# Merge gate A interleaved with the recurrence heads, the last head's gates in the GeLU gate

## The chip, the cores and the metric

The kernel runs on one core of a Trainium2 chip. The metric is the device time of one execution in microseconds (us). The engines are named as the profile names them: PE is TensorE's matmul row (PEld its weight loads), DVE is VectorE, ACT is ScalarE, POOL is GpSimd, SP issues most of the transfers.

## The reference

One layer of a diffusion backbone on 512 latent tokens and 256 context tokens, width 1024, all in fp32. What matters here is the token mixer, and in it the columns of one combined projection:

```python
z_lat = einsum('btd,de->bte', h_lat, w_in)   # columns: Fourier | X | GeLU gate G | merge gate A | merge gate B
u = dwconv(z[..., X])                        # width 4, per channel, latent and context
r = sigmoid(einsum('bthi,hij->bthj', u, wa) + ba)     # 8 heads of 128 channels, 2 directions
i = sigmoid(einsum('bthi,hij->bthj', u, wi) + bi)
log_a = -8 * r * softplus(-lam);  a = exp(log_a)
b = sqrt(-expm1(2 * log_a)) * (i * u)
h_t = a_t * h_{t-1} + b_t                    # scans: context, then latent; forward and backward
y_rnn  = (gelu(z[..., G]) * (h_fwd + h_bwd)) @ w_lru
merge  = sigmoid(z[..., A]) * y_four + sigmoid(z[..., B]) * y_rnn
x      = x + g1 * (merge @ w_out)            # g1 from the adaLN modulation of c
```

After it come the routing and 16 SwiGLU experts (expert choice, 64 tokens each), and a final RMSNorm.

## The kernel before, in words

The program is written out by hand for each engine: every engine runs its instructions in the order in which the code issues them, and waits on semaphores between engines.

**Weights.** The mixer's weights come as tiles of 256 columns (1 MB, list `W`), in the order Fourier, four X tiles, four A tiles, four G tiles, and so on. `load_next()` issues the next transfer of the list `seq` on SP's queue into one of three `raw` buffers. `split(j)` makes two parts of a tile, a rounded one `wH` (a copy on ACT, or on DVE where the caller says so) and the rest `wL` (a subtraction on DVE), each in two halves. There are two buffers for `wH` and two for `wL`. Every product of the mixer is three matmuls per 128 rows of the contraction (`mm3`): high by high, high by low, low by high.

**Recurrence.** For each of the 8 heads `h` the code issues the X columns of the head (`zX`, L725 and L726: 24 matmuls of 512 latent columns and 24 of 256 context columns, in 8 steps `k`), then `conv(h)` on DVE, which makes `u`. The four gate products of the head *before* (`gate(h - 1, ...)`, L674 and L675, plain fp32) stand behind steps k = 4, 5, 6 and 7 of `zX`. Each gate product is followed by a Tanh on ACT (L677). Then `lru(h - 1)`: on ACT two Tanh, two Exp and two Sqrt, on DVE two products with `u` (L688), two products with the root (L698), on POOL two products (L699), on DVE three scans (L705 to L709), on POOL the sum into `yr` (L711). In even heads the split of the next X tile, with its copies on DVE, stands between the products and the scans.

**Merge gate A.** Behind all heads: 8 column tiles `zA` of 24 matmuls (L426), each ended by `a_evac`: a Tanh on ACT and a product into `y4` on DVE (L751). The gate products of the last head stand in the second of these tiles, `lru(7)` behind the fourth. Then the GeLU gate: 8 tiles `zG`, each ended by a GeLU on ACT, a product into `yr`, a rounded copy `gH` on ACT and a subtraction `gL` on DVE. Then merge gate B with the recurrent map, the output projection with the routing, and the experts, whose weights (768 KB a transfer) are fetched ahead into rings of buffers.

**adaLN.** Sixteen of the 24 column groups of the modulation are formed between the tiles: `ada_acc` reads one 1 MB tile and makes on DVE two partial sums of 8 products (L271, L273, L276). A later `ada_red` adds them up over the partitions with two matmuls (`adb`, L291), and DVE adds the result to `g1` (L293) and scales it (L294).

**PSUM.** Matmul results lie in four buffers of 128 x 1024 fp32: tag `z` has two (`zX`, half of the `zA` and `zG`), tag `g` two (gate products, `adb`, the other tiles). A tile in a buffer waits until the readers of the tile before it in that buffer are done. The builder picks the buffer when the code opens the tile.

Of the kernel before, what the change touches and what calls it, by code (L numbers as in the profile page):

```python
# [17 lines left out]
P = 128  # L18
D = 1024
# [57 lines left out]
def layer(ctx: ExitStack, tc: tile.TileContext, I, out):  # L77
# [18 lines left out]
    # ------------------------------------------------------------------ long-lived tiles  # L96
# [49 lines left out]
    # ------------------------------------------------------------------ weight stream of the mixer  # L146
# [6 lines left out]
    W += [(cols(w_in, D_F + 256 * i), 8) for i in range(4)]  # L153
    W += [(cols(w_in, D_F + 2 * D + 256 * i), 8) for i in range(4)]
# [5 lines left out]
    J_X, J_A, J_G, J_B, J_O = 2, 6, 10, 14, 22  # L160
# [4 lines left out]
    ada_at = {j: [p] for j, p in zip([J_A] + list(range(J_A + 2, J_O)), range(8, 23))}  # L165
    ada_at[J_O + 1] = [23]
# [133 lines left out]
    # ------------------------------------------------------------------ start: tokens, constants, adaLN of layer input  # L300
# [131 lines left out]
    # ------------------------------------------------------------------ constants of the recurrence  # L432
# [26 lines left out]
    # ------------------------------------------------------------------ Fourier columns, as the modulation arrives  # L459
# [84 lines left out]
    # ------------------------------------------------------------------ 2-D DFT of the Fourier group, by its symmetries  # L544
# [73 lines left out]
    # ------------------------------------------------------------------ Fourier map to the model width  # L618
# [28 lines left out]
    # ------------------------------------------------------------------ recurrent branch  # L647
# [65 lines left out]
    GATES = [(0, 0), (0, 1), (1, 0), (1, 1)]  # L713
    AT = {4: 0, 5: 1, 6: 2, 7: 3}
    load_gw(0)
    for h in range(H):
        if h % 2 == 0:
            w = SP.pop(J_X + h // 2)
        zf = f2(zt(f"zX{h}"))
        for k in range(KD):  # L720
            wH, wL = ch(w, k, h % 2)
            n = 0
            for a, b, bc in ((wH, hH, cH), (wH, hL, cL), (wL, hH, cH)):
                f, l = k == 0 and n == 0, k == KD - 1 and n == 2
                pe.matmul(zf[:, 512:1024], a, b[:, k, :], start=f, stop=l)  # L725
                pe.matmul(zf[:, 256:512], a, bc[:, k, :], start=f, stop=l)  # L726
                n += 1
# [25 lines left out]
    def last_gates(k):  # L753
        if k % 2:
            gate(H - 1, *GATES[k // 2])
        if k == 1:
            a_evac(0, zz_[0])
        if k == 4:
            split(J_A + 1)

    for i in range(4):
        w = SP.pop(J_A + i) if i < 2 else use(J_A + i)
        zz_ = []
        for c in range(2):
            z = ct(c if i else 0, "zA")
            zz_.append(z)
            zcols(w, z, c, None if i or c == 0 else last_gates)
        evacs = lambda: [a_evac(2 * i + c, zz_[c]) for c in range(0 if i else 1, 2)]
        if i == 1:
            lru(H - 1, pre=lambda: split(J_A + 2, dve.tensor_copy), mid=evacs)  # L770
            close_lr()
            close_hc()
        else:
            evacs()
# [561 lines left out]
```

## Time and profile before

| | |
|---|---|
| time of three runs | 1219.57 us median (1216.5, 1219.57, 1226.09) |
| span of the profiled execution | 1215.1 us, 4.5 us under the median; a time of its own is not listed |
| mean granted TensorE clock | 0.987 of full speed |
| busy share of the span | PE 94%, PEld 56%, DVE 46%, ACT 24%, POOL 9% |
| bytes read from HBM | 364.43 MB, 302 GB/s over the span |
| X columns and recurrence | 96.6 to 215.7 us |
| merge gate A | 215.7 to 273.1 us |
| GeLU gate | 273.1 to 319.7 us |
| gate B and recurrent map; output and routing | 319.7 to 412.6; 412.6 to 475 us |
| experts and final norm | 475 to 1215 us |

The stage times are the starts of the first matmul of each stage on the timeline, from the span's start. A share of busy time is a mean over stages that have different limits, so each stage is to be read by itself.

### The profile page before, as it was taken

How to read it: one execution, taken by the hardware profiler on the slowest of the kernel's cores; microseconds unless marked ns; L12 is line 12 of the kernel's file. 1: busy time of each engine (PE TensorE's matmuls, PEld its weight loads, DVE VectorE, ACT ScalarE, POOL GpSimd, SP SyncE). 2: the span in 40 equal slices, each digit the busy share in tenths (PEclk: the TensorE clock that was granted, in tenths of full speed). 3: DMA queues.
4: the chain of work that ended last, by engine and by line, in shares of the span. 5: the costliest groups of instructions: out<-in, count | busy, mean ns of one | idle time of the engine just before them, and what ended most of it. 6: DMA issues, size and time to landing. Idle time of an engine off the chain costs nothing. (4 is left out here: it accounts for less than half of the span.)

```text
span 1215.1 us, 16698 instructions
## 1 busy us (share of the span) xinstructions
PE 1145.7 (94%) x6873; PEld 684.3 (56%) x6891; DVE 564.3 (46%) x1053; ACT 286.2 (24%) x448; POOL 112.7 (9%) x118
## 2 busy tenths in 40 slices
PE   8989988899999999999999999999999899999886
PEld 4768766688888897545445454344344344344333
DVE  5556899987666665232332342232232232232024
ACT  5543777634322222101001001001001001001004
POOL 4254343210000000000000000000000000000002
PEclk9989988999999999999999999999999999999999
DMA  8912011154664595999999999999999999999996
GB/s 310 318 62 91 21 45 53 49 183 150 207 199 148 181 395 213 314 387 416 364 408 417 403 407 418 403 408 419 409 410 418 413 413 414 410 414 411 404 399 212
DMA packets 146155, 368.01 MB, mean 303 GB/s; under 512 B 8912, under 2 KB 61656, under 8 KB 145952
## 3 DMA queue, kind: packets, MB, share of 16 engines
q1 hardware_dynamic: 143408, 363.52, 78.1%
q0 software_dynamic: 1088, 2.18, 0.6%
q10 hardware_dynamic: 1584, 1.25, 0.4%
q8 instruction: 54, 0.88, 0.3%
q14 instruction: 21, 0.17, 0.0%
HBM read 364.43 MB, written 2.10 MB: 302 GB/s over the span
## 5 line engine op out<-in xcount | busy, mean ns | idle before, releaser
L1111 PE MATMUL U<-ew,g 128*64 128x384 f32 x928 | 168.6, 495 | 10.4 <-DMA ew<-in_w_up_e 10.0
L1111 PE MATMUL G<-ew,g 128*64 128x384 f32 x960 | 174.5, 493 | 2.1 <-DMA ew<-in_w_gate_e 1.6
L1130 DVE TENSOR_TENSOR x<-x,sc 128x512 f32<-128x512 f32 x120 | 77.1, 684 | 101.9 <-PE sc L1127 101.9
L1111 PEld LDWEIGHTS U<-ew,g 128*64 128x64 f32 x928 | 59.6, 136 | 93.9 <-issue 55.0
L1111 PEld LDWEIGHTS G<-ew,g 128*64 128x64 f32 x960 | 65.7, 136 | 81.2 <-issue 60.2
L1244 POOL TENSOR_TENSOR o<-x,ew 128x512 f32<-128x512 f32 (+1 forms) x8 | 7.8, 1004 | 938.2 <-ACT o L1240 938.2
L1206 PE MATMUL Y<-ew,wd 128*64 128x512 f32 x324 | 82.8, 595 | 5.6 <-DMA ew<-in_w_down_e 5.5
L1210 DVE SCALAR_TENSOR_TENSOR wc<-Y,gc,g 128x512 f32<-128x512 f32 x15 | 11.3, 751 | 160.5 <-PE Y L1206 160.5
L1206 PE MATMUL Y<-ew,wa 128*64 128x512 f32 x312 | 78.1, 599 | 7.8 <-DMA ew<-in_w_down_e 4.6
L1194 ACT COPY wa<-T 128x384 f32<-128x384 f32 x16 | 7.7, 479 | 255.4 <-PE T L1193 255.4
L230 DVE TENSOR_TENSOR wL<-raw,wH 128x1024 fp32r<-128x1024 f32 x48 | 62.9, 1340 | 2.0 <-ACT wH L229 1.6
L1206 PEld LDWEIGHTS Y<-ew,wd 128*64 128x64 f32 x324 | 24.3, 137 | 56.5 <-issue 41.5
L1167 ACT ACTIVATE wc<-G 128x768 f32<-128x768 f32 x16 | 13.0, 811 | 178.8 <-PE G L1111 178.8
L1083 PEld LDWEIGHTS xg<-wa,xn 128*128 128x128 f32 x448 | 51.1, 192 | 0.2
L1083 PE MATMUL xg<-wa,xn 128*128 128x128 f32 x448 | 51.2, 275 | 0.0
L1206 PEld LDWEIGHTS Y<-ew,wa 128*64 128x64 f32 x312 | 23.5, 136 | 48.6 <-issue 31.7
L1049 DVE TENSOR_SCALAR wc<-wa,score 128x128 bf16<-128x128 f32 (+3 forms) x63 | 23.9, 379 | 57.0 <-ACT wa L1042 57.0
L1213 ACT CAST wb<-wc 128x512 fp32r<-128x512 f32 x15 | 9.3, 617 | 169.3 <-DVE wc L1210 169.3
L674 PE MATMUL ga<-u,gw 128*128 128x512 f32 x64 | 36.0, 645 | 10.0 <-issue 9.9
L1127 PEld LDWEIGHTS sc<-wb 64*128 64x128 f32 x240 | 23.9, 184 | 35.9 <-issue 35.3
L229 ACT CAST wH<-raw 128x1024 fp32r<-128x1024 f32 x38 | 38.0, 1045 | 18.3 <-PE zO L426 9.9
L699 POOL TENSOR_TENSOR th<-tp,th 128x768 f32<-128x768 f32 x16 | 35.0, 2205 | 49.2 <-DVE tp L698 49.2
(360 smaller groups left out, 2191.2 us busy)
## 6 DMA issues: line engine op xcount, KB each, us to landing
ew<-in_w_gate_e SPq DMA_DIRECT2D x120, 768.0 KB, 13.3
ew<-in_w_up_e SPq DMA_DIRECT2D x116, 768.0 KB, 15.0
ew<-in_w_down_e SPq DMA_DIRECT2D x113, 768.0 KB, 15.0
raw<-in_w_ada SPq DMA_DIRECT2D x24, 1024.0 KB, 5.5
raw<-in_w_in SPq DMA_DIRECT2D x16, 1024.0 KB, 4.8
wd<-in_w_down_e SPq DMA_DIRECT2D x7, 768.0 KB, 12.5
we<-in_w_down_e SPq DMA_DIRECT2D x7, 768.0 KB, 12.9
wd<-in_w_up_e SPq DMA_DIRECT2D x6, 768.0 KB, 14.6
```

What stands on the lines that cost most here:

```text
L229: (copy or act.copy)(wH[:, a], raw[:, a])
L230: dve.tensor_sub(wL[:, a], raw[:, a], wH[:, a].bitcast(F32))
L674: pe.matmul(gf[:, 512:1024], gw[:, d, i, :], u[:, TC:TA], start=True, stop=True)
L699: pool.tensor_tensor(b, s, b, op=OP.mult)
L1049: dve.tensor_scalar(GT[c][:, 0:m], sB[:, 0:m], s, None, op0=OP.is_lt)
L1083: pe.matmul(a[k // 4][:, P * (k % 4) + q.start:P * (k % 4) + q.stop], XN[n // 2][:, n % 2, P * k:P * k + P], oh[:, n, q], start=n == 0, st ...
L1111: pe.matmul(t[64 * f:64 * f + 64, n, 0:384], xg[:, k, c:c + CAP], w[:, o:o + 384], start=k == 0, stop=k == KD - 1, tile_position=(0, 64 * f))
L1127: pe.matmul(a[dh][:, c], w, v, start=j == 0, stop=j == 1, tile_position=(64 * dh, 0))
L1130: dve.tensor_add(xs, xs, a[dh])
L1167: act.activation(v3(sl), G[:, :, 0:384], AF.Silu)
L1206: pe.matmul(yp[64 * dh:64 * dh + 64, :], hT[j // 3][:, j % 3, 64 * f:64 * f + 64], w[dh][:, i, :], start=kf == 0, stop=kf == 11, tile_posi ...
L1210: dve.scalar_tensor_tensor(y, yp, gc[:, e % 3:e % 3 + 1], g2, op0=OP.mult, op1=OP.mult)
```

## The change

The weight tiles are ordered X, A, X, A, ... Behind the X columns of head `h` follows one A tile of 128 columns, `zA[h]`, in a `g` buffer. Its `a_evac` stands behind step k = 3 of the next head's X columns, ahead of that head's gate products. The gate products of the last head stand in the first GeLU tile behind k = 1, 3, 5 and 7, its `a_evac` behind k = 0, and `lru(7)` behind that tile. All splits now copy on ACT; the split of an A tile stands at the head of an even head, that of the next X tile behind `conv` of an odd head. `ada_red` and `ada_acc` stand at the end of each odd head, behind `lru(h - 1)`, and then behind each pair of GeLU tiles as before; all 16 groups are done one place or more earlier, so that one `ada_red` and one `ada_acc` in the output projection fall away.

```diff
     W = [(cols(w_in, 256 * i), 8) for i in range(2)]
-    W += [(cols(w_in, D_F + 256 * i), 8) for i in range(4)]
-    W += [(cols(w_in, D_F + 2 * D + 256 * i), 8) for i in range(4)]
+    for i in range(4):
+        W.append((cols(w_in, D_F + 256 * i), 8))
+        W.append((cols(w_in, D_F + 2 * D + 256 * i), 8))
...
-    ada_at = {j: [p] for j, p in zip([J_A] + list(range(J_A + 2, J_O)), range(8, 23))}
-    ada_at[J_O + 1] = [23]
+    ada_at = {j: [p] for j, p in zip([J_X + 1, J_X + 3, J_X + 5, J_X + 7] + list(range(J_G, J_O)), range(8, 24))}
...
+    zA = {}
+
+    def tail_of(h, k, at):
+        if k == at[0] - 1:
+            a_evac(h, zA.pop(h))
+        if k in at:
+            gate(h, *GATES[at.index(k)])
...
     for h in range(H):
         if h % 2 == 0:
-            w = SP.pop(J_X + h // 2)
+            split(J_X + h + 1)
+            wx, wg = SP.pop(J_X + h), SP.pop(J_X + h + 1)
...
-            if h and k in AT:
-                gate(h - 1, *GATES[AT[k]])
+            if h:
+                tail_of(h - 1, k, (4, 5, 6, 7))
...
         conv(h, zf[:, 256:1024])
-
-        def next_split(h=h):
-            if h % 2 == 0:
-                split(J_X + h // 2 + 1, dve.tensor_copy)
+        if h % 2:
+            split(J_X + h + 1)
+        zA[h] = gt("zA")[:, 0, :]
+        zcols(wg, zA[h], h % 2)
         if h:
-            lru(h - 1, next_split)
-        else:
-            next_split()
+            lru(h - 1)
+        if h % 2:
+            ada_red()
+            ada_acc(J_X + h)
...
     for i in range(4):
         w = use(J_G + i)
         for c in range(2):
             z = ct(c, "zG")
-            zcols(w, z, c)
             j = 2 * i + c
+            zcols(w, z, c, None if j else lambda k: tail_of(H - 1, k, (1, 3, 5, 7)))
+            if j == 0:
+                lru(H - 1)
...
         if n == 1:
             ada_red()
-            ada_acc(J_O + 1)
...
-    ada_red()
```

DVE, `lru(3)` before, from the products with the root to the next `conv` (`tp3` and `th` are its tiles, `wL5` is the next weight tile):

```order
L698 SCALAR_TENSOR_TENSOR tp3_1385<-th0_3_1339,tp3_1385 128x768
L698 SCALAR_TENSOR_TENSOR tp3_1388<-th0_3_1361,tp3_1388 128x768
L229 CAST wH5_1399<-raw17_884 128x1024
L230 TENSOR_TENSOR wL5_1400<-raw17_884,wH5_1399 128x1024
L229 CAST wH5_1399<-raw17_884 128x1024
L230 TENSOR_TENSOR wL5_1400<-raw17_884,wH5_1399 128x1024
L705 SCALAR_TENSOR_TENSOR tp3_1385<-th0_3_1339,th1_3_1350 128x768
L707 SCALAR_TENSOR_TENSOR tp3_1388<-th0_3_1361,th1_3_1372 128x256
L709 SCALAR_TENSOR_TENSOR tp3_1388<-th0_3_1361,tp3_1388,th1_3_1372 128x512
L663 TENSOR_SCALAR u5_1483<-zX5_1411,col_80 128x768
```

The split stands ahead of the scans, and the next `conv` right behind them.

DVE in the changed program, `lru(2)`, which stands in odd head 3, from the same place on (`adb8` is the sum over the partitions, `acc9` the next `ada_acc`):

```order
L698 SCALAR_TENSOR_TENSOR tp2_1422<-th0_2_1343,tp2_1422 128x768
L698 SCALAR_TENSOR_TENSOR tp2_1425<-th0_2_1365,tp2_1425 128x768
L705 SCALAR_TENSOR_TENSOR tp2_1422<-th0_2_1343,th1_2_1354 128x768
L707 SCALAR_TENSOR_TENSOR tp2_1425<-th0_2_1365,th1_2_1376 128x256
L709 SCALAR_TENSOR_TENSOR tp2_1425<-th0_2_1365,tp2_1425,th1_2_1376 128x512
L293 TENSOR_TENSOR g1_94<-adb8_1440,g1_94 128x256
L294 TENSOR_SCALAR g1_94<-g1_94 128x256
L271 TENSOR_SCALAR acc9_0_1444<-raw20_1171,cs_91 128x256
L271 TENSOR_SCALAR acc9_1_1445<-raw20_1171,cs_91 128x256
```

The read of `adb8` now stands behind the scans. Six more `acc9` products, `L276`, both halves of the next A tile's `wL7`, the product `y4_3` of `zA[3]` and `conv(4)` follow in this order.

PE, the first gate product of the last head (`ga7`) before, in the second A tile (the semaphores that a row waits on are in brackets):

```order
L426 MATMUL zA_1735<-hH_99,wH6_1603 128x512 [waits DVE_49,PE_49]
L426 MATMUL zA_1735<-hL_100,wH6_1603 128x512
L426 MATMUL zA_1735<-hH_99,wL6_1604 128x512
L426 MATMUL zA_1735<-hH_99,wH6_1603 128x512
L426 MATMUL zA_1735<-hL_100,wH6_1603 128x512
L426 MATMUL zA_1735<-hH_99,wL6_1604 128x512
L674 MATMUL ga7_1742<-u7_1684,gw7_1578 128x512 [waits DMASW0_49,Activation_49]
```

Here the A tile waits for DVE (the `conv` that reads the same buffer), and the gate product for a Tanh on ACT.

PE in the changed program, the same product in the first GeLU tile, behind `zA[7]` and `adb10`:

```order
L291 MATMUL adb10_2003<-acc10_1_1728,ones_86 128x256 [waits Activation_49]
L426 MATMUL zG_2028<-hH_99,wH10_1952 128x512 [waits Activation_49]
L426 MATMUL zG_2028<-hL_100,wH10_1952 128x512
L426 MATMUL zG_2028<-hH_99,wL10_1953 128x512 [waits DVE_49]
L426 MATMUL zG_2028<-hH_99,wH10_1952 128x512
L426 MATMUL zG_2028<-hL_100,wH10_1952 128x512
L426 MATMUL zG_2028<-hH_99,wL10_1953 128x512
L674 MATMUL ga7_2037<-u7_1944,gw7_1819 128x512 [waits DMASW0_49,DVE_49]
```

The gate product now lies in the `g` buffer that `adb10` had, and its wait on DVE is for `g1<-adb10`; the other `g` buffer holds `zA[7]`.

The buffers of tag `g` that the builder picked (0 or 1, in the order of opening): head 2: gates 0 0 0 0, `zA[2]` 1. Head 3: gates 0 1 0 1, `zA[3]` 0, `adb8` 1. Head 4: gates 1 1 1 0, `zA[4]` 1. Heads 5 and 7 are as head 3 (`adb9` and `adb10` in 1), head 6 as head 4. In the GeLU gate: gates 1 1 0 1, the second GeLU tile 0, `adb11` 1, the fourth GeLU tile 0. So in head 4, 6 and the GeLU gate the first gate product waits for the read of `adb`, and in heads 3, 5 and 7 the second one for the `y4` product of the A tile before.

## Rows read from the trace of the kernel before

**Rows 1.** Windows by stage: length, busy us by engine, granted clock, DMA share, GB/s.

```profile
core 0: us, PE busy (x) PEld busy (x) DVE busy (x) ACT busy (x) POOL busy (x), PEclk, DMA share, GB/s
96.60:215.70 119.10, 109.05 (x499) 82.54 (x498) 100.33 (x107) 71.54 (x76) 49.92 (x39) 0.94 0.17 54
215.70:273.10 57.40, 52.96 (x215) 40.61 (x213) 50.93 (x64) 29.79 (x35) 12.27 (x7) 0.97 0.37 121
273.10:319.70 46.60, 46.60 (x206) 37.78 (x204) 34.35 (x66) 18.08 (x25) 0.00 (x0) 1.00 0.54 180
412.60:475.00 62.40, 61.44 (x534) 56.65 (x535) 40.38 (x96) 18.54 (x35) 0.00 (x0) 1.00 0.65 248
475.00:1215.00 740.00, 697.37 (x4494) 329.63 (x4508) 222.13 (x500) 72.94 (x150) 7.77 (x8) 1.00 1.00 395
```

**Rows 2.** Timeline of PE: start, length, instruction, idle time before it in brackets.

```profile
65.60 1.09 PE L556 MATMUL fb<-dc,zs 128*128 128x65 f32 x4 [5.81 <-DVE zs L495]
...
138.91 1.10 PE L674 MATMUL ga<-u,gw 128*128 128x512 f32 x2 [0.99 <-issue]
...
150.90 0.40 PE L725 MATMUL zX<-hH,wH 128*128 128x512 f32 x1
...
151.96 0.39 PE L725 MATMUL zX<-hH,wH 128*128 128x512 f32 x1
...
157.63 2.05 PE L674 MATMUL ga<-u,gw 128*128 128x512 f32 x2 [4.46 <-issue]
...
225.86 0.47 PE L426 MATMUL zA<-hH,wH 128*128 128x512 f32 x1 [4.19 <-DVE u L667]
...
256.05 0.40 PE L426 MATMUL zA<-hH,wH 128*128 128x512 f32 x1
...
261.65 0.40 PE L426 MATMUL zA<-hH,wH 128*128 128x512 f32 x1
```

**Rows 3.** Windows behind three of these waits.

```profile
65.60:73.10 7.50, 7.50 (x32) 6.48 (x32) 3.53 (x13) 3.73 (x8) 5.77 (x22) 0.50 0.00 1
139.00:140.00 1.00, 1.00 (x3) 0.52 (x4) 1.00 (x2) 1.00 (x1) 0.00 (x0) 1.00 0.00 0
157.63:162.16 4.53, 4.53 (x10) 3.03 (x11) 3.46 (x4) 4.49 (x5) 1.33 (x1) 0.51 0.00 0
162.16:164.50 2.34, 2.34 (x12) 1.68 (x11) 1.25 (x1) 1.31 (x2) 2.34 (x2) 1.00 0.00 0
```

**Rows 4.** Timelines of DVE and ACT, the first head's recurrence.

```profile
117.71 1.08 DVE L663 TENSOR_SCALAR u<-zX,col 128x768 f32<-128x768 f32 x1 [4.27 <-PE zX L726]
...
121.97 1.82 DVE L688 SCALAR_TENSOR_TENSOR th<-th,u 128x768 f32<-128x768 f32 x2
...
133.29 1.28 DVE L709 TENSOR_TENSOR_SCAN tp<-th,tp,th 128x512 f32<-128x512 f32 x1
...
119.00 0.91 ACT L677 ACTIVATE th<-ga,lru_c 128x768 f32<-128x768 f32 x1 [1.44 <-PE ga L675]
```

**Rows 5.** Timelines of DVE and ACT in merge gate A.

```profile
258.47 0.40 DVE L293 TENSOR_TENSOR g<-adb,g 128x256 f32<-128x256 f32 x1
...
259.99 2.35 DVE L230 TENSOR_TENSOR wL<-raw,wH 128x1024 fp32r<-128x1024 f32 x2
262.26 1.27 DVE L751 SCALAR_TENSOR_TENSOR y<-zA,y 128x512 f32<-128x512 f32 x2
263.46 0.60 DVE L271 TENSOR_SCALAR acc<-raw,cs 128x256 f32<-128x256 f32 x2
...
266.82 2.35 DVE L230 TENSOR_TENSOR wL<-raw,wH 128x1024 fp32r<-128x1024 f32 x2
...
262.35 1.99 ACT L229 CAST wH<-raw 128x1024 fp32r<-128x1024 f32 x2
```

**Rows 6.** Timelines of ACT and DVE in the GeLU gate, one tile's end.

```profile
284.68 0.58 ACT L787 ACTIVATE zG<-zG 128x512 f32<-128x512 f32 x1 [2.72 <-PE zG L426]
...
285.30 0.69 DVE L788 TENSOR_TENSOR yr<-zG,yr 128x512 f32<-128x512 f32 x1 [2.61 <-ACT zG L787]
...
286.02 0.62 ACT L789 CAST gH<-yr 128x512 fp32r<-128x512 f32 x1 [0.76 <-DVE yr L788]
```

More of the change, by code (lines that the diff above doesn't have):

```diff
@@ L159, in layer @@
     W += [(cols(I["w_out"][0], 256 * i), 8) for i in range(4)]
-    J_X, J_A, J_G, J_B, J_O = 2, 6, 10, 14, 22
+    J_X, J_G, J_B, J_O = 2, 10, 14, 22
     NW = len(W)
@@ L711, in lru @@
         pool.tensor_tensor(yr[:, h, :], tps[0][:, TC:TA], tps[1][:, TC:TA], op=OP.add)
[L713 to L716, printed above, removed]
-        if h % 2 == 0:
-            w = SP.pop(J_X + h // 2)
[L719 to L727, printed above, removed]
-            if h and k in AT:
-                gate(h - 1, *GATES[AT[k]])
-        if h + 1 < H:
-            load_gw(h + 1)
-        conv(h, zf[:, 256:1024])
-        def next_split(h=h):
-            if h % 2 == 0:
-                split(J_X + h // 2 + 1, dve.tensor_copy)
-        if h:
-            lru(h - 1, next_split)
-        else:
-            next_split()
     def zcols(w, o, c, tick=None):
@@ L751, in a_evac @@
         dve.scalar_tensor_tensor(y4[j][:, :], z, 1.0, y4[j][:, :], op0=OP.add, op1=OP.mult)
[L753 to L774, printed above, removed]
-        ada_red()
-        ada_acc(J_A + i)
-    gp, close_gp = sb("gp", "right")
-    gH = gp.tile([P, H, T], F32R, name="gH")
-    gL = gp.tile([P, H, T], F32R, name="gL")
+    GATES = [(0, 0), (0, 1), (1, 0), (1, 1)]
+    zA = {}
[4 more added lines that the diff above has]
+            gate(h, *GATES[at.index(k)])
+    load_gw(0)
+    for h in range(H):
+        if h % 2 == 0:
+            split(J_X + h + 1)
+            wx, wg = SP.pop(J_X + h), SP.pop(J_X + h + 1)
+        zf = f2(zt(f"zX{h}"))
+        for k in range(KD):
+            wH, wL = ch(wx, k, h % 2)
+            n = 0
+            for a, b, bc in ((wH, hH, cH), (wH, hL, cL), (wL, hH, cH)):
+                f, l = k == 0 and n == 0, k == KD - 1 and n == 2
+                pe.matmul(zf[:, 512:1024], a, b[:, k, :], start=f, stop=l)
+                pe.matmul(zf[:, 256:512], a, bc[:, k, :], start=f, stop=l)
+                n += 1
+            if h:
+                tail_of(h - 1, k, (4, 5, 6, 7))
+        if h + 1 < H:
+            load_gw(h + 1)
+        conv(h, zf[:, 256:1024])
+        if h % 2:
+            split(J_X + h + 1)
+        zA[h] = gt("zA")[:, 0, :]
+        zcols(wg, zA[h], h % 2)
+        if h:
+            lru(h - 1)
+        if h % 2:
+            ada_red()
+            ada_acc(J_X + h)
     for i in range(4):
@@ L784, in layer @@
             z = ct(c, "zG")
-            zcols(w, z, c)
             j = 2 * i + c
+            zcols(w, z, c, None if j else lambda k: tail_of(H - 1, k, (1, 3, 5, 7)))
+            if j == 0:
+                lru(H - 1)
+                close_lr()
+                close_hc()
+                gp, close_gp = sb("gp", "right")
+                gH = gp.tile([P, H, T], F32R, name="gH")
+                gL = gp.tile([P, H, T], F32R, name="gL")
             act.activation(z, z, AF.Gelu_apprx_tanh)
@@ L944, in layer @@
     dve.tensor_copy(bias, g[:, 0, 0:NE])
-    ada_red()
     dve.tensor_mul(wr[:, :, 0:NE], wr[:, :, 0:NE], s2.unsqueeze(2).to_broadcast([P, KD, NE]))
```

## The prediction

> **What bounds the kernel now.** I read the windows by stage first, then PE's timeline in the stages that the change touches, then the engines that PE waits for there.
>
> In the last stage, 740 us of experts, the DMA engines are busy all the time (share 1.00, 395 GB/s) and PE 697 us of it [rows 1]. The change touches nothing there, and its transfers are issued behind the first part of the output projection. So the question is only when the mixer ends; what is won or lost in it moves the end by as much.
>
> The stages of the X columns, gate A and the GeLU gate last 119.1 + 57.4 + 46.6 = 223.1 us. PE is the engine that is nearly full in all three, but it waits [rows 2]: per pair of heads 0.99 us in one and 4.46 us in the other, where a gate product needs `u` and DVE has not come to that `conv` (the 4.46 comes twice, one row stands), and 4.19 us at the second A tile, whose buffer `conv` still reads. After the long waits the granted clock is at half, 1.2 of 2.4 GHz, for a while: a gate product and an X step take 4.53 us, where the next pair takes 2.34 [rows 3], so each costs 2.2 more. That is 0.99 + 2 x 4.46 + 4.19 = 14.1 us of waits and 3 x 2.2 = 6.6 us of slow clock, **20.7 us** in all. It is the most that a better order of the same work can win here.
>
> **The work itself does not change.** An X step of six matmuls takes 151.96 - 150.90 = 1.06 us, so the X columns of a head 8.5; a gate product 2.34 - 1.06 = 1.28; an A or GeLU tile of 24 matmuls 261.65 - 256.05 = 5.60 [rows 2, 3]. A pair of heads with two A tiles and one `adb` (about 0.4, an estimate from its 256 fp32 columns beside the gate's 768) is 2 x (8.5 + 5.1 + 5.6) + 0.4 = 38.8 us. What counts is which waits stand in it.
>
> **What a wait is now made of.** The recurrence of one head is a chain through four engines. It starts when the X columns end (117.71, where `conv` starts), the last Tanh of the gates starts 1.3 later, and the last scan ends at 134.57: **16.9 us** after the X columns [rows 4]. DVE's own work ahead of it, `conv` and the products with `u`, is 4.3 + 1.8, and a split 2.3 [rows 4, 5]: 8.4, less than the chain needs to reach DVE, so the chain sets the time and not DVE's load. In an odd head the changed program puts two copies of a split on ACT ahead of this chain, 1.99 us [rows 5]: 18.8. Then comes the read of `adb`, 0.4 [rows 5]: **19.2 us** after the X columns of an odd head. In an even head no copy stands ahead: 16.9, and the `y4` product, 0.6 [rows 5], ends at **17.5**.
>
> **Odd head to even head (3 to 4, 5 to 6).** From the end of X(3) PE runs the fourth gate product 1.3, `zA` 5.6, `adb` 0.4 and five X steps 5.3: 12.6. There stands the first gate product, whose buffer was `adb`'s: it waits until 19.2, **6.6 us**, and everything behind it on PE, the other X steps, waits with it. The slow clock follows, 2.2. Three gates and three steps, 7.0, later X(4) ends, at 28.4. The fourth gate waits for `y4_3`, which is behind `ada_acc` (263.46 to 266.82, 3.4), a split (2.3) and its own 0.6 [rows 5]: 25.5, hidden.
>
> **Even head to odd head (4 to 5, 6 to 7).** 1.3 + 5.6 + 5.3, then the first gate and a step, 2.3: 14.5. The second gate waits for `y4_4` until 17.5: **3.0 us**. Whether the clock falls after it no row tells: after 0.99 us it stayed at full speed, after 4.46 it fell [rows 2, 3]. I take none: 3.0 is the difference of two long sums, and the shorter row kept its clock; the other end is 2.2. So a pair has 6.6 + 2.2 + 3.0 = 11.8 us of waits, where a pair before has 0.99 + 4.46 + 2.2 = 7.7; two pairs give 23.6.
>
> **Heads 1 to 3.** There is no `adb` yet, but `y4_1` stands behind scans 18.8, `ada_acc` 3.4 and a split 2.3: 25.1. PE comes to `zA[2]`, whose buffer it is, at 1.3 + 5.6 + 8.5 + 5.1 = 20.5, a wait of 4.6. `conv(2)` stands behind `y4_1` too, so the chain of that head is 3.8 late, and the second gate of head 3 waits another 2.2: **6.8 us**. The slow clock after the first wait would only shorten the second.
>
> **GeLU gate.** From the end of X(7): 1.3 + 5.6 + 0.4 and two steps of 0.7 = 8.7, then the gate that needs `adb10` read: 19.2, **10.5 us**, and 2.2 of slow clock. The third gate needs `y4_7` at 25.5 and comes later, 26.8: hidden. The fourth gate ends at 30.8, and `lru(7)`, with no X columns left to lie beside, 15.6 after that (119.00 to 134.57) at 46.4. The product of the first tile, its copy (285.30 to 286.64), the GeLU of the second (0.6) and its product (0.7) [rows 6] end at 49.0. PE has done the second tile and the third by 30.8 + 5.6 + 0.4 + 5.6 = 42.4, and the fourth lies in the second's buffer: **6.6 us**, and 2.2. Together 21.5.
>
> **What else moves.** In the output projection one `ada_acc` and one `adb` fall away; PE is busy 61.4 of 62.4 us there [rows 1], so only the `adb` counts, 0.5 us. `raw` transfers: three per pair of heads instead of mostly one, on a queue whose engines are busy 0.17 to 0.37 [rows 1], each issued a head or more ahead; no cost. POOL's own order is the same; a split no longer lies beside POOL's products, which shortens DVE's load and not the chain.
>
> **Sum.** New waits 6.8 + 23.6 + 21.5 = 51.9; old ones gone 20.7; 0.5 off: **+30.7 us**. The profiled span would be 1215.1 + 30.7 = 1245.8 us. It is 4.5 us below the median of the three runs, so against the median 1219.57 + 30.7 = **1250 us**.
>
> **Bounds.** If the clock came back at once behind all four long waits, 8.8 less: 1241. If it stayed low as after the 5.81 us wait (7.5 us at 0.50, 3.75 lost instead of 2.2 [rows 2, 3]), 6.2 more, and with the clock low after the two waits of 3.0 us 4.4 more: 1261.
>
> **Rival 1: the A tiles cover the recurrence, and it is faster.** All 20.7 + 0.5 us are won: 1198 us. It decides itself at one point: whether `adb` is read within 12.6 us of the odd head's X columns and `y4` within 14.5 of the even one's. For it: DVE has less to do per pair than PE (two times conv 4.3, products 3.6, scans about 5.2, split 2.3 and `y4` 0.6, with 0.4 and 3.4 for adaLN: 36 against 38.8), and the wait for `conv` is gone indeed, since 5.6 us of `zA` stand ahead of it. Against it: the two waits hang on the end of the chain, 16.9 us, which no load shortens. The Trainium skill (Perfetto Trace Analysis, Optimization Strategy) says that where the most-contended engine changes from regime to regime, interleaving the regimes may help; DVE is busy 100 of 119 us in the first and PE 53 of 57 in the second, and by this rule the time is this rival's. The same page (Matmuls) says that independent groups should rotate through different PSUM banks, so that the reading of one overlaps with the next; the 4.19 us wait bears it out, and it speaks against this order, where `adb`, `zA` and the gates share two buffers. With a free buffer for each the sum would be rival 1's as well.
>
> **Rival 2: smaller, but slower.** The builder's buffers hold, but the chain is shorter than in the first head, by 3 us: then 6.6 becomes 3.6 twice, 3.0 nothing twice, 10.5 becomes 7.5, and the clock falls less often: some 12 + 4 us less, 1234. What speaks against it is that the chain was measured in a head where nothing else was queued.
>
> **Rival 3: the delay is lost behind.** If the experts' weights were fetched as early as before, a late mixer would find full buffers, and PE, which has 740 - 697 = 43 us of slack there, could catch up: no change, 1219. Against it: these transfers are issued behind the mixer's own work, and 395 GB/s with a share of 1.00 leaves nothing to catch up with.
>
> **How the numbers follow.** The forecast as walked, with its bounds from 1241 to 1261, has 0.78; rival 2 0.10; rival 1 0.07; rival 3 0.05. Within 1%, 12 us, is about what a measurement of this kernel can tell from no change. Faster comes from rival 1; same from rival 3; slower from the rest. The range takes the bounds and half of rival 2: 1233 to 1263.
>
> **What would show it.** From the first `zX` to the first `zB` some 254 us instead of 223. Waits of PE: the gate product for DVE's `g1` at L293, two times about 6.6 and once about 10.5; for `y4` at L721, about 3 us in heads 3, 5 and 7, and `zA[2]` 4.6; the fourth `zG` about 6.6 for `yr`. Clock at half behind the long ones. No wait for `u`. The expert stage as long as before. I am wrong if the waits on L293 are absent or near 1 us, or if the stretch to `zB` is long but the end does not move.

## The result and the profile after

The changed kernel takes 1261.61 us (median of 4 runs, 1258.42 to 1261.98), the kernel before 1218.55 in the same session: ratio 1.0341, 95% interval 1.0311 to 1.0372, so 43 us slower. The profiled execution took 1261.37 us with a span of 1259.3, 44.2 more than the span before. The forecast was +30.7.

The two traces by stage, from the first `zX`, `zB` and `zO` and the last `zO` (us):

| | before | after | difference | forecast |
|---|---|---|---|---|
| up to the first `zX` | 96.7 | 98.8 | +2.1 | 0 |
| first `zX` to first `zB` (X columns, gate A, GeLU gate) | 223.0 | 259.4 | +36.4 | +31.2 |
| first `zB` to first `zO` | 93.0 | 93.0 | 0 | 0 |
| output projection, first to last `zO` | 55.0 | 60.6 | +5.6 | -0.5 |
| the rest (experts) | 747.4 | 747.5 | +0.1 | 0 |

The 2.1 us at the start are no effect of the change: the first `zX` began anywhere from 95.5 to 102.3 us in the executions profiled below. The windows of the changed kernel (length, busy us of PE, PEld, DVE, ACT, POOL, granted clock, DMA share, GB/s) for the X columns with gate A, the GeLU gate, the output projection and the experts answer to [rows 1]:

```profile
98.80:283.50 184.70, 160.70 (x695) 122.59 (x694) 129.16 (x158) 94.50 (x104) 50.90 (x40) 0.93 0.23 74
283.50:358.20 74.70, 56.93 (x224) 43.87 (x223) 51.80 (x79) 32.88 (x41) 10.89 (x6) 0.89 0.36 121
451.20:519.10 67.90, 64.33 (x533) 59.39 (x532) 36.80 (x86) 18.54 (x35) 0.00 (x0) 0.95 0.55 213
519.10:1259.10 740.00, 698.47 (x4510) 329.70 (x4508) 222.22 (x500) 72.87 (x150) 7.76 (x8) 1.00 1.00 395
```

The experts take the same 740 us at 395 GB/s: what the mixer lost is lost at the end. PE stands idle 24 us of the first stage and 18 of the GeLU gate, which had no idle time before, and the granted clock is 0.93, 0.89 and, in the output projection, 0.95, where it was 0.94 to 1.00 in these stages before.

PE's timeline of the changed kernel (start, length, instruction, idle time before it and what ended it) has these waits from the X columns to gate B, where [rows 2] had those for `u`:

```profile
140.66 1.12 PE L674 MATMUL ga<-u,gw 128*128 128x512 f32 x2 [0.80 <-ACT th L677]
151.43 0.79 PE L426 MATMUL zA<-hH,wH 128*128 128x512 f32 x1 [4.10 <-DVE y L721]
191.44 2.08 PE L674 MATMUL ga<-u,gw 128*128 128x512 f32 x2 [6.53 <-DVE g L293]
218.16 1.47 PE L674 MATMUL ga<-u,gw 128*128 128x512 f32 x2 [3.02 <-DVE y L721]
243.87 2.08 PE L674 MATMUL ga<-u,gw 128*128 128x512 f32 x2 [6.53 <-DVE g L293]
271.62 1.12 PE L674 MATMUL ga<-u,gw 128*128 128x512 f32 x2 [3.02 <-DVE y L721]
295.69 2.08 PE L674 MATMUL ga<-u,gw 128*128 128x512 f32 x2 [10.40 <-DVE g L293]
326.69 0.79 PE L426 MATMUL zG<-hH,wH 128*128 128x512 f32 x1 [7.38 <-DVE yr L776]
```

The waits for `u` are gone, as forecast, and in their place stand those of the forecast: `zA[2]` 4.10 (4.6), the first gate of heads 4 and 6 6.53 (6.6), the second gate of heads 5 and 7 3.02 (3.0), the first gate in the GeLU gate 10.40 (10.5), the fourth `zG` 7.38 (6.6). Only the 2.2 that the forecast had in head 3 did not come, and 0.80 in head 2 was not in it. They sum to 41.8 us, 27.7 more than the 14.1 before.

DVE's timeline of an odd head of the changed kernel shows the row in which the readers of PE's buffers stand. `conv(3)` starts at 172.34, when the X columns end:

```profile
189.78 1.28 DVE L709 TENSOR_TENSOR_SCAN tp<-th,tp,th 128x512 f32<-128x512 f32 x1
190.99 0.40 DVE L293 TENSOR_TENSOR g<-adb,g 128x256 f32<-128x256 f32 x1
191.42 1.14 DVE L294 TENSOR_SCALAR g<-g 128x256 f32<-128x256 f32 x1
...
193.01 2.45 DVE L273 SCALAR_TENSOR_TENSOR acc<-raw,cs,acc 128x256 f32<-128x256 f32 x6
...
195.83 2.35 DVE L230 TENSOR_TENSOR wL<-raw,wH 128x1024 fp32r<-128x1024 f32 x2
198.10 0.68 DVE L721 SCALAR_TENSOR_TENSOR y<-zA,y 128x512 f32<-128x512 f32 x1
```

The last scan ends at 191.06, 18.7 us after the X columns (forecast 18.8), `adb` is read at 191.39, and PE's gate starts at 191.44. The `y4` product ends at 198.78, 26.4 after the X columns, where the forecast had 25.5.

The windows behind the waits answer to [rows 3], at PE's granted clock (the first number after the busy times):

```profile
151.43:157.38 5.95, 5.95 (x14) 4.69 (x15) 5.91 (x10) 4.65 (x5) 0.00 (x0) 0.50 0.81 272
191.44:194.92 3.48, 3.48 (x7) 2.17 (x8) 3.48 (x8) 0.52 (x1) 0.97 (x1) 0.50 0.00 0
218.82:222.24 3.42, 3.42 (x11) 2.44 (x10) 0.00 (x0) 0.91 (x1) 0.06 (x1) 0.50 0.00 0
243.87:249.54 5.67, 5.67 (x12) 3.66 (x13) 5.63 (x12) 0.91 (x1) 0.97 (x1) 0.50 0.03 9
271.62:275.00 3.38, 3.38 (x13) 2.24 (x14) 0.00 (x0) 0.90 (x1) 0.71 (x1) 1.00 0.00 0
295.69:300.74 5.05, 5.05 (x10) 3.35 (x11) 5.02 (x11) 0.90 (x1) 0.97 (x1) 0.50 0.00 0
326.69:331.46 4.77, 4.77 (x11) 3.80 (x12) 4.10 (x11) 2.98 (x4) 0.00 (x0) 0.50 0.00 0
477.67:485.00 7.33, 7.33 (x37) 7.33 (x38) 3.13 (x5) 0.00 (x0) 0.00 (x0) 0.54 0.87 337
```

Up to gate B PE runs 28.3 us at half clock (the six windows with 0.50), a loss of 14.2, where the forecast had 8.8. With it the stretch is explained: 27.7 of waits + 14.2 - 6.6 of slow clock before = 35.3 of 36.4.

The last window is in the output projection, where nothing was foreseen. There `pb` is the first matmul that reads the router's weights `wr`. The timelines of SP and ACT, of before and then of after, show the issue of `wr` and of the first experts' weights `ew`; PE's row of the changed kernel stands last:

```profile
418.68 0.55 SPq L202 DMA_DIRECT2D raw<-in_w_ada  x1
423.39 0.38 SPq L190 DMA_DIRECT2D raw<-in_w_out  x1
423.81 3.88 SPq L856 DMA_DIRECT2D ew<-in_w_gate_e  x7
419.41 0.39 ACTq L863 DMA_DIRECT2D wr<-in_w_router  x1
```

```profile
457.47 0.37 SPq L190 DMA_DIRECT2D raw<-in_w_out  x1
457.89 5.12 SPq L844 DMA_DIRECT2D ew<-in_w_gate_e  x7
458.20 0.39 ACTq L851 DMA_DIRECT2D wr<-in_w_router  x1
477.67 3.06 PE L930 MATMUL pb<-wr,modc 128*128 128x16 f32 x16 [2.67 <-DMA wr<-in_w_router]
```

Before, an adaLN weight took the `raw` buffer that came free at 418.68; the last output weight waited until 423.39 for the next one, and SP came to the experts only 4.4 us after `wr` was issued, which landed 5.1 us after its issue. After, that adaLN weight is gone from SP's row, the last output weight takes the free buffer, and 7 transfers of 768 KB follow it, the first 0.3 us ahead of `wr`. The 64 KB are there some 19.5 us after their issue, by the end of PE's wait. PE waits 2.67 and then loses 3.4 of 7.33 us at clock 0.54: 6.0, about the 5.6 of the table.

### The profile page after: what moved, and what is told of

Its sections match the earlier page's. It is cut to its first block, busy times and chain, and to the rows that moved or that the text cites. A ratio compares the mean times of both kernels' runs of the same rounds, so it can differ in the third digit from the quotient of the medians.

```text
span 1259.3 us, 16718 instructions
## 1 busy us (share of the span) xinstructions
PE 1159.7 (92%) x6891; PEld 693.3 (55%) x6891; DVE 556.8 (44%) x1043; ACT 293.9 (23%) x457; POOL 112.4 (9%) x118
## 5 line engine op out<-in xcount | busy, mean ns | idle before, releaser
L230 DVE TENSOR_TENSOR wL<-raw,wH 128x1024 fp32r<-128x1024 f32 x48 | 58.2, 1251 | 1.6 <-ACT wH L229 1.6
L229 ACT CAST wH<-raw 128x1024 fp32r<-128x1024 f32 x48 | 47.9, 1045 | 17.8 <-PE zO L426 9.9
L677 ACT ACTIVATE th<-ga,lru_c 128x768 f32<-128x768 f32 x32 | 28.9, 902 | 88.0 <-PE ga L675 88.0
L1113 PEld LDWEIGHTS sc<-wb 64*128 64x128 f32 x240 | 23.9, 184 | 35.9 <-issue 35.3
## 6 DMA issues: line engine op xcount, KB each, us to landing
we<-in_w_down_e SPq DMA_DIRECT2D x7, 768.0 KB, 12.4
```

What stands on the lines that cost most here:

```text
L229: (copy or act.copy)(wH[:, a], raw[:, a])
L230: dve.tensor_sub(wL[:, a], raw[:, a], wH[:, a].bitcast(F32))
L677: act.activation(t, gf[:, 256:1024], AF.Tanh, bias=(hbi if i else hba)[:, 8 * d + h:8 * d + h + 1], scale=0.5)
L1113: pe.matmul(a[dh][:, c], w, v, start=j == 0, stop=j == 1, tile_position=(64 * dh, 0))
```

## The experiments

Ratios are against the kernel before in the same session (its medians 1219.35, 1219.46, 1219.8 and 1219.91), differences to the changed kernel against 1261.6. These differences cross sessions, between which the kernel before moved by up to 1.4 us (1218.55 to 1219.91). The stage times are those of each run's profiled execution.

| run | median us | ratio, 95% interval | `zX` to `zB` | output projection |
|---|---|---|---|---|
| changed kernel | 1261.61 | 1.0311 to 1.0372 | 259.4 | 60.6 |
| e1_router | 1256.33 | 1.0274 to 1.0315 | 258.6 | 54.6 |
| e5_ada (from before) | 1228.06 | 1.0046 to 1.0099 | 225.4 | 62.4 |
| e2_adb | 1248.67 | 1.0223 to 1.0255 | 244.8 | 60.4 |
| e3_y4 | 1233.87 | 1.0103 to 1.0147 | 231.8 | 60.4 |
| e4_both | 1234.96 | 1.0097 to 1.0155 | 232.3 | 61.0 |
| e8_gates_only | 1253.07 | 1.0206 to 1.0314 | 249.8 | 59.1 |
| e6_gates | 1231.58 | 1.0060 to 1.0119 | 229.7 | 60.4 |
| e10_even | 1222.60 | 1.0012 to 1.0043 | 222.2 | 60.5 |
| e11_warm | 1266.77 | 1.0348 to 1.0411 | 262.8 | 62.5 |
| e7_all | 1211.26 | 0.9907 to 0.9949 | 216.7 | 54.6 |
| e9_last | 1211.88 | 0.9918 to 0.9960 | 215.9 | 54.6 |
| e12_shift | 1209.77 | 0.9903 to 0.9944 | 210.3 | 54.6 |

### The output projection: e1_router and e5_ada

```diff
 e1, in the changed kernel
-    nc.scalar.dma_start(wr[:, :, 0:NE], I["w_router"][0].rearrange("(k p) e -> p k e", p=P))
+    nc.sync.dma_start(wr[:, :, 0:NE], I["w_router"][0].rearrange("(k p) e -> p k e", p=P))
 e5, in the kernel before
-    ada_at = {j: [p] for j, p in zip([J_A] + list(range(J_A + 2, J_O)), range(8, 23))}
-    ada_at[J_O + 1] = [23]
+    ada_at = {j: [p] for j, p in zip(range(J_A, J_O), range(8, 24))}
...
-            ada_acc(J_O + 1)
...
-    ada_red()
```

> The changed kernel, with the 64 KB load of the router's weights issued on SP's queue, ahead of the experts' weights, instead of on ACT's. Theory: the output projection is 5.5 us longer because SP is free earlier there (no adaLN weight stands in its row any more), so 7 expert transfers are issued 0.3 us ahead of the router's load and this one lands after them; PE waits 2.7 us for it and then runs at half clock. Expected: no wait of PE for wr, first zO to last zO 54 to 55 us instead of 60.3, the total 5 to 6 us below the changed kernel, about 1256. Rival: the end is set by the experts' transfers, which are issued at the same moment as before, so PE's wait in the output projection is made up behind it: the total stays at 1261.

> The kernel before, with one part of the change alone: the last adaLN weight is accumulated in merge gate A instead of in the output projection. Theory: SP has no adaLN weight to wait for in the output projection, issues the experts' weights before ACT issues the router's load, and PE waits for that load with a slow clock behind it. Expected: a wait for wr of 2 to 4 us in the output projection, first zO to last zO 59 to 61 us instead of 54.8, total 4 to 6 us above before, about 1223 to 1225. Rival: the move is free or saves the 0.5 us of adb on PE, as the prediction had it, and the 5.5 us belong to something else in the changed order: 1218 to 1219.

With the load ahead on SP's queue, `pb` no longer waits, the output projection takes 54.6 us, and the total falls by 5.3: the theory's 5 to 6. SP's timeline of this kernel:

```profile
458.95 0.37 SPq L851 DMA_DIRECT2D wr<-in_w_router  x1
459.37 5.01 SPq L844 DMA_DIRECT2D ew<-in_w_gate_e  x8
```

The other way round, moving the adaLN weight alone makes the kernel before 8.7 us slower, more than the 4 to 6 expected. PE's timeline of it shows why:

```profile
446.86 3.57 PE L941 MATMUL pb<-wr,modc 128*128 128x16 f32 x16 [3.45 <-DMA wr<-in_w_router]
```

The wait for `wr` is there, 3.45, and the output projection is 7.4 longer; 2.4 more lie in gate A, where one more weight is accumulated and PE waits 1.66 for it at an `adb` (267.83). Both runs say that the loss there is the order of issue of two transfers, made by a part of the change that removes work.

### What stands behind the scans: e2_adb, e3_y4, e4_both

What is given to `lru` as `mid` is issued between its products and its scans; `evac` is the Tanh and the `y4` product of an A tile.

```diff
 e2
         if h:
-            lru(h - 1)
+            lru(h - 1, mid=ada_red if h % 2 else None)
         if h % 2:
-            ada_red()
             ada_acc(J_X + h)
 e3: y4 alone (no a_evac in tail_of)
+        evac = lambda: a_evac(h, zA.pop(h))
-            lru(h - 1)
+            lru(h - 1, mid=lambda: (evac()))
 e4: y4 and adb
+            lru(h - 1, mid=lambda: (evac(), ada_red() if h % 2 else None))
```

> The changed kernel, with the read of adb moved on DVE ahead of the scans of the odd heads; y4 stays behind them. Theory: the waits come from all that is queued behind the scans, not from adb alone. With adb read about 13.2 us after the X columns the first gate of heads 4 and 6 waits only 0.7 us instead of 6.5, but then zA of that head comes at 20.9 us to a buffer that y4 gives back at 25.5 (4.6 us), conv of the next head stands behind that y4 as well, and the second gate of the next odd head waits 4.3 instead of 3.0: 9.6 us a pair, as now. In the GeLU gate 10.4 becomes some 4.5 at the first gate and some 8 for y4 at the fourth. Expected: waits for L293 under 6 us in all instead of 23.5, those for L721 up from 10 to 25 to 32 us, total within 8 us of the changed kernel's 1261. Rival: adb's place behind the scans is itself the cause: 13 + 10.4 us and the slow clock behind them go, total 1228 to 1235.

> The changed kernel, with the Tanh and the y4 product of each A tile moved ahead of the scans of the head that runs beside it; adb stays behind the scans. Theory: the order of DVE's queue costs more than PE's waits by line say. zA[2]'s wait (4.1 and slow clock) and the two of 3.0 go; the first gate of heads 4 and 6 now gets the buffer of y4 (ready about 13.3 us after the X columns, 12.6 when PE comes), and adb's buffer is wanted by the third gate, at 17.3 against 19.4: 2 us instead of 6.5. In the GeLU gate 4.6 for y4 and about 5 for adb instead of 10.4, and 7 for yr as now. Expected: 22 to 30 us below the changed kernel, 1231 to 1239. Rival: each wait belongs to its own line, so only those for y4 go (4.1 + 6.0 and 4.6 of slow clock): 1247. Second rival: DVE becomes the bound of a pair of heads, conv comes late, and less than 10 us are won.

> The changed kernel, with the y4 product of each A tile and, in odd heads, the read of adb ahead of the scans (the two moves of the earlier experiments together). Theory: with y4 moved, what is left of the waits for adb is small (1.6 us where y4 alone was moved), and now DVE's queue is the limit: the split of the A weights comes late by 6.0 us in three places, and reading adb ahead of the scans makes DVE's odd head no shorter. Expected: within 4 us of the kernel with y4 alone moved, 1230 to 1238, with PE waiting for wL at L230. Rival: the two moves add up, 13 us more as adb alone brought: 1221.

With `adb` alone moved, 12.9 us are won, more than the 8 at most expected and less than half of what the rival had. PE's timeline of that kernel in heads 4 and 5, and DVE's in head 5:

```profile
197.83 0.79 PE L426 MATMUL zA<-hH,wH 128*128 128x512 f32 x1 [4.15 <-DVE y L721]
213.15 1.12 PE L674 MATMUL ga<-u,gw 128*128 128x512 f32 x2 [0.41 <-DVE y L721]
```

```profile
203.68 1.82 DVE L698 SCALAR_TENSOR_TENSOR tp<-th,tp 128x768 f32<-128x768 f32 x2
```

The wait moved on to `y4`, as the theory had it (4.15 against 4.6), but the second gate of the next head hardly waits (0.41 against 4.3): `conv(4)` starts late, at 197.69, and `y4_4` ends at 213.10, 15.4 us later and not 17.5. ACT had run ahead meanwhile: DVE goes into L698 without a wait, where in the changed kernel it waited 1.97 us for ACT at this place (208.72). POOL had not; it waits for DVE in both. So part of a delay on DVE is made up in the next head, which neither theory had. The waits for `y4` sum to 15.8 us, where the theory had 25 to 32.

With `y4` alone moved, 27.7 us are won, in the expected range and over the first rival's. Moving both wins no more (1235.0 against 1233.9). PE's timeline of e4 around head 4, and DVE's:

```profile
182.08 1.12 PE L674 MATMUL ga<-u,gw 128*128 128x512 f32 x2 [0.75 <-DVE y L721]
193.30 0.50 PE L426 MATMUL zA<-hH,wL 128*128 128x512 f32 x1 [2.17 <-DVE wL L230]
```

```profile
189.19 2.46 DVE L273 SCALAR_TENSOR_TENSOR acc<-raw,cs,acc 128x256 f32<-128x256 f32 x6
...
192.03 2.35 DVE L230 TENSOR_TENSOR wL<-raw,wH 128x1024 fp32r<-128x1024 f32 x2
```

The first gate, now in the buffer of an A tile, finds it within 0.75 us, and now `zA` waits 2.17 for its own weights' split, which stands behind `ada_acc`. So the second rival of e3, DVE as the bound, is there too, but small. No run gave the gates, `zA` and `adb` a buffer each, which the prediction names as another way to the same end; that stays untested.

### The last head's gates: e8_gates_only and e6_gates

```diff
+        last = None
+        if h == H - 1:
+            def last(k):
+                if k == 3:
+                    lru(h - 1)
+                if k >= 4:
+                    gate(h, *GATES[k - 4])
-        zcols(wg, zA[h], h % 2)
+        zcols(wg, zA[h], h % 2, last)
 GeLU gate, first pair of tiles: both zcols, then
+            lru(H - 1, mid=lambda: (product(0), product(1)))
 product(c) is the GeLU and the product with yr; e6 has e4's moves as well
```

> The changed kernel, with the second part of the change undone: the last head's gates run in its own A tile (after X step 3 of it), its recurrence beside the first two GeLU tiles, whose products with yr stand ahead of its scans; the X, A order and the places of y4 and adb stay. Theory: the 10.4 us wait for adb and the 7.4 for yr with their slow clock (22.7 in all) go, but DVE has both recurrences of the last heads, an adaLN weight and three splits in a row there, so zG1 waits some 1.5 us for y4, zG2 as much for its split, and zG4 some 6 us for the split of its weights, with the clock low behind it: 8 to 14 us won, 1247 to 1254. Rival: the GeLU gate's loss was the place of these gates alone, and all 22.7 go: 1239. Second rival: the recurrence of the last head is only moved, and nothing is won: 1258 to 1262.

> All three moves in one: y4 and adb ahead of the scans, and the last head's gates in its own A tile. Theory: against the kernel with y4 and adb moved the GeLU gate loses its waits for y4, adb and yr (about 16 us with the slow clock) and gets one for the split of zG4's weights (6 and slow clock): 1218 to 1226. Rival: DVE is the bound from the last X columns to the end of the GeLU gate, and no more than 4 us are won over the two moves alone.

e8 gives 8.5 us, inside the expected 8 to 14, though its four runs lie 15 us apart (1243.1 to 1258.1), and it is there by luck and not by the theory: `zG1` and `zG4` do not wait, and the waits for `adb` and `yr` are gone, but PE waits 6.17 us at the second of these gates. In e6 the same wait stands, and only 3.4 us are won over e4 (the intervals overlap), which is the rival's figure, though its cause (DVE) was another. ACT's timeline of e6:

```profile
263.51 1.28 ACT L695 ACT_TABLE_LOAD   x1
264.80 1.58 ACT L695 ACTIVATE tp<-tp 128x768 f32<-128x768 f32 x2
266.39 1.28 ACT L677 ACT_TABLE_LOAD   x1
267.69 0.90 ACT L677 ACTIVATE th<-ga,lru_c 128x768 f32<-128x768 f32 x1
```

I had put head 6's recurrence ahead of head 7's gates on ACT; the first gate's Tanh, whose buffer the second gate needs, stands behind all of it and two table loads. A row on ACT did what DVE's did in the changed kernel.

### Where adaLN is accumulated: e10_even and e7_all

```diff
-    ada_at = {j: [p] for j, p in zip([J_X + 1, J_X + 3, J_X + 5, J_X + 7] + ...
+    ada_at = {j: [p] for j, p in zip([J_X, J_X + 2, J_X + 4, J_X + 6] + ...
-        if h % 2:
+        if h % 2 == 0:
             ada_acc(J_X + h)
 e10: e4 with this; e7: e6 with this and with e1's edit
```

> The kernel with y4 and adb ahead of the scans (1235), and the adaLN weights of the heads accumulated in even heads instead of odd ones; the gates of the last head stay in the GeLU gate and the router's load on ACT's queue. Theory: the waits of three A tiles for the split of their weights (7.7 us) stood behind the 3.4 us of ada_acc in DVE's row; with it moved they go, and with them what PE loses behind: 8 to 13 us, 1222 to 1227. Rival: DVE's sum per pair is the same, so the waits move to conv or y4 of the other head: 1231 to 1235.

> As the one before, and the adaLN weights of the heads accumulated in even heads (DVE has 16.5 us of work there and 26 in odd ones), and the router's load on SP's queue ahead of the experts' weights. Theory: the router's load gives 5.3 as it did alone, and the evened load takes away most of the waits for the split of A weights, 3 to 8 us: 1206 to 1216, under the kernel before. Rival: DVE's sum over a pair of heads is what counts, not how it is spread, so only the router's 5.3 are won: 1214 to 1220, no different from before.

e10 is 12.4 us under e4, at the good end of what was expected: no tile waits for `wL` any more, and from first gate to first gate a pair of heads takes 39.85 us (135.41, 175.26, 215.12), where the forecast counted 38.8 of PE's work. e7 has it with the router's load and the gates in gate A: 1211.26, 20.3 under e6, of which the output projection's 5.8 is e1's. Its time lies in the expected range by luck: that range was set while e6 was expected at 1218 to 1226 and the edit at 8 to 13 us, and both were off. The 16.5 and 26 us of the expectation are the lengths of DVE's row in an even and an odd head; its work there in e4 is 13.6 and 23.0. e7 is the first that beats the kernel before, by 0.7%.

### Is it the clock: e11_warm

```diff
+            if h in (4, 6) and k == 4:
+                warm(26, zt("warm"))
             if h:
                 tail_of(h - 1, k, (4, 5, 6, 7))
 and warm(42, zt("warm")) ahead of the first gate in the GeLU gate
```

> The changed kernel, with matmuls on a constant put ahead of the three gate products that wait for adb (26 in heads 4 and 6, 42 in the GeLU gate, some 0.22 us each): they fill most of the 6.5, 6.5 and 10.4 us in which PE stands still and compute nothing that is used. Theory: the clock falls because PE stands still there, and the time lost behind these waits (1.75, 2.7 and 2.5 us, half of the stretch at half clock) comes back: 5 to 7 us below the changed kernel, 1254 to 1257. Rival: what follows is set by the recurrence's chain and not by PE's clock, so a faster PE only waits longer at the next place: 1260 to 1262.

The time came out above both ranges: 1266.8, 5.2 over the changed kernel. PE's timeline of this kernel in heads 4 to 7, and then the third gate product of head 4 in the changed kernel:

```profile
194.61 1.12 PE L674 MATMUL ga<-u,gw 128*128 128x512 f32 x2 [0.85 <-DVE g L293]
202.01 1.12 PE L674 MATMUL ga<-u,gw 128*128 128x512 f32 x2 [2.24 <-DVE y L721]
222.14 2.07 PE L674 MATMUL ga<-u,gw 128*128 128x512 f32 x2 [3.00 <-DVE y L721]
...
276.75 2.08 PE L674 MATMUL ga<-u,gw 128*128 128x512 f32 x2 [3.00 <-DVE y L721]
```

```profile
198.02 1.13 PE L674 MATMUL ga<-u,gw 128*128 128x512 f32 x2
```

The clock stayed at 1.00 through the filled waits, but in heads 4 and 6 the run does not test the theory, because with the edit the tiles lie in other buffers. The third gate product waits 2.24 us for `y4` at 202.01; in the changed kernel it started at 198.02, before that `y4` product ended (198.78), so there it cannot have lain in the same buffer. From first gate to first gate, heads 4 and 5 take 54.6 us instead of 52.4 and heads 6 and 7 54.6 instead of 51.8. Part of this is the third gate's wait; the rest is the clock, which in this execution fell behind both waits of 3.00 (0.50 in windows of 3.86 and 4.25 us from 222.14 and 276.75), where in the changed kernel it fell behind one of two.

In the GeLU gate the third gate product shares its buffer with `y4` in both kernels. There PE, with the clock kept up, comes earlier and waits 1.78 for `y4` and again 7.38 for `yr`, so that from the first gate to the fourth `zG` it takes 30.7 us instead of 31.0: of the 2.5 that the window of 5.05 us had cost, 0.3 came back. So the rival is right there; what the slow clock costs in heads 4 and 6 stays open. Of the whole, `zX` to `zB` is 3.4 longer, and 1.9 are in the output projection, which this edit does not touch: it took 60.4 to 62.5 us in the runs from the changed kernel that left the router's load as it was and the last gates in the GeLU gate.

### Toward a better order: e9_last and e12_shift

The diff shows the main lines.

```diff
 e9: e10 with e1's edit; the first pair's products ahead of lru(H - 1)'s scans, and
+            zcols(w, z[c], c, None if i or c else lambda k: tail_of(H - 1, k, (4, 5, 6, 7)))
 e12: e9 with one adaLN weight less in the GeLU gate
-    zip([J_X, J_X + 2, J_X + 4, J_X + 6] + list(range(J_G, J_O)), range(8, 24))
+    zip([J_X, J_X + 2, J_X + 4, J_X + 6] + list(range(J_G + 1, J_O)), range(8, 23))
+    ada_at[J_B] = [15, 16], the later ones one place on
+            if i + c == 0:
+                ada_red()
+                ada_acc(J_B)
```

> The fastest so far (1211), with the last head's gates back in the first GeLU tile, at its last four steps, and the products of the first two GeLU tiles still ahead of that head's scans. Theory: in its own A tile these gates waited 4.3 and 1.6 us for ACT, which has the head before's recurrence in its row; in the GeLU tile they wait some 3 us for y4, the 7.4 for yr do not come back, and zG4 may wait up to 2.7 for its split: 2 to 6 us won, 1205 to 1209. Rival: the last head's recurrence then starts 6 us later, and the GeLU gate waits for it as in the changed kernel: 1214 to 1218.

> The kernel before this one (1212, gates in the first GeLU tile), with one adaLN weight taken out of the GeLU gate: the first of the four is accumulated one place later, and merge gate B, where DVE is busy 29 of 42 us, takes two in its first pair of tiles. Theory: the wait of 5.6 us at the small adb product of the GeLU gate (PE waits for ada_acc, which stands behind the last head's scans and two gL products on DVE) goes, and DVE comes to the split of zG4's weights 3.4 us earlier: 4 to 8 us won, 1204 to 1208. Rival: DVE's backlog at the end of the recurrence is what counts, and the wait moves to a split, a product with yr or gate B: 1209 to 1213.

e9 is no faster than e7. The wait for `yr` did not come back, so the rival is wrong too; PE waits 2.55 for `y4` as expected and then 5.61 for an adaLN weight's sum, which no theory named and which e10 has too (6.98). Its timeline, then that of e12:

```profile
258.80 1.13 PE L674 MATMUL ga<-u,gw 128*128 128x512 f32 x2 [2.55 <-DVE y L721]
288.70 1.01 PE L287 MATMUL adb<-ones,acc 128*128 128x1 f32 x4 [5.61 <-DVE acc L276]
```

```profile
286.98 0.50 PE L429 MATMUL zG<-hH,wH 128*128 128x512 f32 x1 [2.39 <-ACT wH L232]
```

e12 takes that wait away, and `zX` to `zB` falls by 5.6 to 210.3 us, but the medians differ by 2.1 only (1209.77 against 1211.88, with overlapping intervals). The time lies in the rival's range. The trace bears out both in part: the named wait is gone, as the theory had it, but `zG` now waits 2.39 for its split, and from `zB` to `zO` it takes 93.9 us instead of 92.9, as the rival had it. Against the kernel before it is 0.9924, 0.9903 to 0.9944: the lowest of all, though e7 and e9 cannot be told from it.

## Why the prediction was right, and where not

- **The mechanism held.** But for the one in head 3, the waits of PE are where the forecast put them and as long, within 0.8 us each, because they hang on the end of a chain that [rows 4, 5] measured: 16.9 + 1.99 forecast, 18.7 measured. e3 and e4 confirm the cause from the other side: with `y4` and `adb` read ahead of the scans, 27 of the 43 us go with the same work on every engine.
- **Size of the clock term.** "2.2" behind each of four long waits made 8.8; these four measured 1.7, 2.8, 2.5 and 2.4, together 9.5. The other 4.7 of the 14.2 come from two windows that the forecast had put at nothing: 5.95 us at half clock behind `zA[2]`'s wait, and 3.42 behind one wait of 3.0. Against the first of them it had set the 2.2 in head 3. That wait did not come, because the recurrence behind the late `conv(2)` took 15.4 us (151.29 to 166.70) and not 17.5, as in e2. The clock is thus 5.4 over the forecast and the waits 1.3 under it; this is most of the 5.2 us by which +36.4 exceeds +31.2, and 1.1 is unexplained. What these microseconds cost by themselves e11 shows in the GeLU gate alone: almost nothing, since PE then waits for other readers.
- **The step that failed** is "only the `adb` counts, 0.5 us" of the output projection. It priced the removed adaLN weight on PE and did not follow it on SP's queue, where it had taken a buffer, so that the last output weight and the experts' weights behind it came 4.4 us after the router's load and not ahead of it: +5.6 instead of -0.5, shown by e1 and e5. The words on `raw` transfers, "no cost", held for the stages before: no wait there names a `raw`.
- **Rival 1's condition was not enough.** It asked that `adb` and `y4` be read in time, and counted on DVE's 36 us against PE's 38.8 per pair. In e4 they are read in time in the heads (0.75 us of waiting is left at each first gate), DVE has 36.6 us of work in heads 3 and 4 as counted, and it is 1235 and not 1198. Of that work 23.0 lie in the odd head and 13.6 in the even one, so three splits come late (3.38, 2.17 and 2.16); and the GeLU gate still waits 4.64 for `y4` and 7.37 for `yr`. With the load evened (e10) a pair takes 39.85, and with the last head's end and the router's load mended (e7, e9, e12) the interleaving is worth 0.6 to 0.8%. The Trainium skill (Perfetto Trace Analysis, Optimization Strategy) says that interleaving may help where the most-contended engine changes from regime to regime. The prediction took DVE for that engine in the first one; by [rows 1] PE is the fullest in both (109.05 of 119.10 us and 52.96 of 57.40), so the sentence does not quite meet this case. The best orders here win 8 to 10 us, once the order within DVE's queue is changed with the interleaving.
- **Rivals 2 and 3** are refuted: the chain was no shorter than in the first head (6.53 us waited, not 3.6; the waits that rival 2 takes off sum to 15 us and not to its 12), and the experts, from the last `zO` to the end, took 747.5 us as before (747.4).
- **The sum.** +31.2 became +36.4, -0.5 became +5.6, and 2.1 lie in the start of this execution: 44.1 of 44.2. The range held 1261.6 near its upper bound, and that is in part luck: of the 11.6 us above the forecast half came from a place that the bounds did not cover.

## What to carry to other kernels

When work is interleaved to cover an engine's wait, list for each rotating buffer who reads it last and what stands ahead of that reader in its own queue: a short read queued behind a recurrence holds the matmul engine for the whole chain, and moving that read ahead of the chain won 27.7 us here. When a step is removed, look at what its waits were holding back, on the DMA queues above all: a small load that others wait for has to be issued ahead of the bulk, by order and not by luck. An engine's load is to be counted per head and not per pair, because it is the fuller half that is late.

## What the runs showed of the hardware

- **A small load behind bulk.** 64 KB issued on ACT's queue landed after 5.1 us beside one weight of 1 MB (issued 0.7 us earlier; DMA share 0.76 from 419.4 to 424.6), and were there after some 19.5 us when 7 transfers of 768 KB went out on SP's queue, the first 0.3 us earlier and the others within 5 us. The Trainium skill (DMA: Bandwidth & Descriptors, Issuing engines are not separate DMA queues) says that transfers issued by different engines share the same 16 DMA engines; the trace agrees.
- **The clock after equal waits.** Behind two waits of 3.02 us in the changed kernel the granted clock was 0.50 in a window of 3.42 us once and 1.00 the other time; in e11 it was 0.50 behind both of 3.00. e1 and e8 repeat the changed kernel: from the start of the first gate 0.58 in 4.0 us, from that of the second 1.00. What PE waited is not enough to tell.
- **DVE beside POOL.** The `tensor_scalar` at L294 (128x256) took 0.30 us in e6 with POOL idle (279.86), 1.14 in the changed kernel and 1.77 in e4, each time beside an instruction on POOL (the sum into `yr`, L711, and a product, L699), and ended 0.15 us after POOL's (192.56 and 192.41, 184.16 and 184.01). The Trainium skill (SBUF — State Buffer, Who interferes with whom) describes an exclusive lock on a port that the two share; the ends agree with it.
